# A hybrid diffusion trunk on one core: last states of a two-way scan left out, and row sums and spread scales by split products

## The chip, the core and the metric

The kernel runs on one core of a Trainium2 chip. The engines are named as the profile names them: PE (TensorE, matrix products), PEld (its weight loads), DVE (VectorE), ACT (ScalarE), POOL (GpSimd) and SP (SyncE, whose queue issues most DMAs). Each engine takes its own instructions in a fixed order, and semaphores make them wait for one another. The metric is the device time of one execution in microseconds (us).

## The reference, cut to what matters

One layer: an HGRN2 mixer (a gated linear recurrence, run forward and backward over the tokens), then a gated ConvFFN, each behind an RMS norm with shift, scale and gate from a conditioning vector. D = 1024, 2048 latent tokens and 256 context tokens, 8 heads of 128, everything float32. The scan, cut to its core:

```python
def hgrn2_chunk_scan(q, k, v, logf, s0):
    # S_t = diag(f_t) S_{t-1} + k_t v_t^T, o_t = S_t^T q_t, in chunks
    ...
    kv = einsum('bhnjk,bhnjv->bhnkv', k * exp(b_last - b), v)
    def step(s, inp):
        dcy, u = inp
        return dcy[..., None] * s + u, s
    s_final, s_start = lax.scan(step, s0, (decay, kv))
    o_inter = einsum('bhnik,bhnkv->bhniv', q * exp(b), s_start)
...
for d in range(2):
    oc_d, s_ctx = hgrn2_chunk_scan(<context, flipped if d>, s0)
    ol_d, _     = hgrn2_chunk_scan(<latents, flipped if d>, s_ctx)
...
sh1, sc1, g1, sh2, sc2, g2 = split(silu(c) @ w_ada + b_ada, 6)
```

A context scan gives its final state to the latent scan of the same direction. The final state of a latent scan (`_`) is read by nothing.

## The kernel before

**Products.** A float32 product of full precision is one PE instruction that the trace shows as two records. The large products are split instead: an operand `x` becomes `h` (an ACT copy rounded to float32r, line L89) and `l = x - h` (DVE, L90), and `x·y` is taken as three fast products `hh`, `hl`, `lh` (`mm3`, L520 to L522). Weights come from HBM into a float32 tile `raw` and are split from there.

**The scan** (`mixer_scan`, about the first 1285 us). Tokens are cut into tiles of 128 (two of context, -2 and -1, and 16 of latents, 0 to 15) and these into six units of three tiles, in two groups: {-2,-1,0}, {1,2,3}, {4,5,6} and {7,8,9}, {10,11,12}, {13,14,15}. The loops run over group, then head, then the three units. For a head, `load_head` brings five weight blocks of 128x1024 (types 1 and 2, the gates of the two directions, into `wh`/`wl`; types 0, 3, 4 into `vh`/`vl`). `unit` emits two gate products (24 matmuls of 384 columns each), q and three value products, and the elementwise scans on DVE. It returns `part_a` and `part_b` for its three tiles s, which are emitted inside the next unit: `part_a` transposes the keys of both directions (`tr`, copied to `kt`) and makes the scores (`sc`), `part_b` makes `kv`, the outputs `o`, and steps the forward state `Sf`; the backward increment `st[:, 2]`, the outputs and the queries go to `stash[t]` in DRAM. Later (`mixer_out`, `heads(t)` for t from 14 down to 0) the backward state `Sb` walks over the stash.

**What else runs in the scan.** `ada_rest` is a generator that makes four rows of the modulation: `acc` sums eight loads `raw` of 128x1024 on DVE, two full-precision products with a column of ones add up the partitions (L782, shape 1x512), ACT copies them to `row` (L783) and a DMA stores it to `m_row` (L784). From head 1 on each unit takes one step of it; a row takes 8 steps, so the products stand behind unit (head 3, 1) and unit (head 6, 0) of each group. `Hidden` prepares the normed tokens of a unit: `total` (`zs`), `root`, `spread0` (a diagonal matrix `dg` of scales) and `spread` (one full-precision product of 384 columns with ones, `zr`, L206).

**The two raw buffers.** The tiles `raw` of the weights and of `ada_rest`, and `row`, share one tag with two buffers in the pool `rawp`: a load may be issued when the tile before the last in that tag has been read for the last time. `wh`/`wl` hold one head: the next head's weights are split into them after the gate products of the head's third unit. A scheduler decides the order of instructions on each engine; SP's queue holds the loads and the stash writes in one order.

Of the kernel before, what the change touches and what calls it, by code (L numbers as in the profile page):

```python
# [10 lines left out]
F32R = mybir.dt.float32r  # L11
# [3 lines left out]
OP = mybir.AluOpType  # L15
# [42 lines left out]
def body(ctx, tc, a, out):  # L58
# [80 lines left out]
    wp = pool_(c1, "wp", 2)  # L139
    hq = pool_(c1, "hq")  # L140
    fix = pool_(c1, "fix")


    PLACE = {("h", 0): 0, ("l", 0): 1, ("h", 1): 2, ("l", 1): 3, ("l", 2): 4, ("h", 2): 5}
# [14 lines left out]
    class Hidden:  # L159
# [40 lines left out]
        def spread0(self):  # L200
            self.dg = self.xp.tile([128, NSC, 128], F32, name="dg", tag="dg")
            diag(self.dg, self.rs)

        def spread(self):
            z = self.ps.tile([128, 1, UN], F32, name="zr", tag="tr")
            pe.matmul(z[:, 0], ones, self.dg.rearrange("p s n -> p (s n)"), start=True, stop=True)  # L206
            self.z = z

        def scaled(self, g):
# [241 lines left out]
    def mixer_scan():  # L451
# [24 lines left out]
        def by_two(m):  # L476

            return m.rearrange("p (a c) b -> p c a b", c=2)

        mx, my, mw = mask("mx"), mask("my"), mask("mw")  # L480
        in_block(mx, 32)
        pool.tensor_copy(mw, mx)
# [41 lines left out]
        def unit(h, w, u, tiles, todo, begun=None, pace=6):  # L524
# [170 lines left out]

            kvb, kts, ats = [], {}, {}

            def part_a(s):
                g4 = slice(4 * s, 4 * s + 4)
                tr = ps.tile([128, 2, 128], F32, name="tr", tag="tr")  # L700
                for d in range(2):
                    pe.transpose(tr[:, d], kd[:, d, g4], ident)
                kt = gp.tile([128, 2, 128], F32, name="kt", tag="kt", bufs=3)
                act.activation(kt, tr, AF.Copy)
                kts[s] = kt
                if s < s0:
                    return

                sc = ps.tile([128, 3, 128], F32, name="sc", tag="sc", bufs=2)
                zig = [[64, 2], [(NS + 1) * 32, 2], [1, 32]]  # L710
                pe.matmul(sc[:, 0], kx[:, g4], walk(qp[:, 0, 4 * s], *zig), start=True, stop=True)
                for d in (1, 0):
                    qx = walk(qp[:, d, 4 * s + 1 - d], [(2 - d) * NS * 32, 2], [64, 2], [1, 32])
                    pe.matmul(sc[:, 2 - d], ke[:, d, g4], qx, start=True, stop=True)
                at = gp.tile([128, 128], F32, name="at", tag="at", bufs=2)
                af, ab = ABs[count["A"] % 2]
                count["A"] += 1
                act.activation(af[64:128, 0:64], sc[64:128, 1, 64:128], AF.Copy)
                act.activation(af[0:64, 64:128], sc[0:64, 2, 64:128], AF.Copy)
                dve.copy_predicated(ab, mxu, sc[:, 0])  # L720
                dve.copy_predicated(by_two(af.rearrange("p (a b) -> p a b", b=32)), myu,
                                    sc[:, 1:3, 0:64].rearrange("p c (a b) -> p c a b", b=32))
                dve.tensor_tensor(at, af, ab, OP.add)
                ats[s] = at

            def part_b(s):
                g4 = slice(4 * s, 4 * s + 4)
                kt = kts[s]
                kv = ps.tile([128, 2, 128], F32, name="kv", tag="kv")
                for d in range(2):  # L730
                    pe.matmul(kv[:, d], kt[:, d], v[:, s], start=True, stop=True)
                if s < s0:
                    kb = gp.tile([128, 3, 128], F32, name="kb", tag="st", bufs=4)
                    act.activation(kb[:, 0], kv[:, 1], AF.Copy)
                    kvb.append(kb[:, 0])
                    if s == 0:
                        dve.tensor_copy(Sf[:, h], kv[:, 0])
                    else:
                        dve.scalar_tensor_tensor(Sf[:, h], Sf[:, h], sd[:, 0, s:s + 1], kv[:, 0],
                                                 OP.mult, OP.add)  # L740
                        dve.scalar_tensor_tensor(Sb[:, h], kvb[1], sd[:, 1, 0:1], kvb[0],
                                                 OP.mult, OP.add)
                    return
                st = sts[s]
                o = ps.tile([128, 128], F32, name="o", tag="o")
                pe.matmul(o, qi[:, 0, g4], Sf[:, h], start=True, stop=False)
                pe.matmul(o, ats[s], v[:, s], start=False, stop=True)
                act.activation(st[:, 0], o, AF.Copy)
                act.activation(st[:, 2], kv[:, 1], AF.Copy)
                dve.scalar_tensor_tensor(Sf[:, h], Sf[:, h], sd[:, 0, s:s + 1], kv[:, 0],  # L750
                                         OP.mult, OP.add)
                t = tiles[s]
                if is_late(h, t):
                    pool.tensor_copy(st[:, 3], qi[:, 1, g4].rearrange("p g t -> p (g t)"))
                    return
                last = h == NH - 1 and t > NT - 4
                q_ = act if last else sp
                q_.dma_start(stash[t][:, 1, h], st[:, 0:2])
                q_.dma_start(stash[t][:, 0, h, 0], st[:, 2])
# [5 lines left out]
        def ada_rest():  # L765

            for i in range(4):
                acc = xp.tile([128, D], F32, name="acc", tag="acc")
                c = i * D
                for k in range(KT):  # L770
                    raw = rawp.tile([128, D], F32, name="raw", tag="raw")
                    sp.dma_start(raw, a["w_ada"][k * 128:(k + 1) * 128, c:c + D])
                    if k == 0:
                        dve.tensor_scalar(acc, raw, sil[:, k:k + 1], None, OP.mult)
                    else:
                        dve.scalar_tensor_tensor(acc, raw, sil[:, k:k + 1], acc, OP.mult, OP.add)
                    if k < KT - 1:
                        yield
                row = rawp.tile([1, D], F32, name="row", tag="raw")
                for n in range(2):  # L780
                    z = ps.tile([1, 512], F32, name="z", tag="pj", bufs=3)
                    pe.matmul(z, ones[:, 0:1], acc[:, n * 512:(n + 1) * 512], start=True, stop=True)  # L782
                    act.activation(row[:, n * 512:(n + 1) * 512], z, AF.Copy)  # L783
                sp.dma_start(m_rows[i], row)  # L784
                yield
# [67 lines left out]
        for g, units in enumerate(GROUPS):  # L853
            for h in range(NH):
# [4 lines left out]
                for u, tiles in enumerate(units):  # L859
# [3 lines left out]
                    if g == 1 and h == NH - 1 and u == 1:  # L863
                        more = last_tile()
                        todo += more[:3]
                    if h > 0 and steps < 16 * (g + 1):
                        next(rest, None)
                        steps += 1
                    if g == h == u == 0:
# [121 lines left out]
    def mixer_out(c3):  # L991
# [9 lines left out]
        def load_stash(i, t):  # L1001

            ko = wk2.tile([128, NH, 2, 128], F32, name=("kq", "og")[i], tag=("kq", "og")[i])
            for hs in ((slice(0, NH),) if t < NT - 3 else (slice(0, NH - 1), slice(NH - 1, NH))):
                sp.dma_start(ko[:, hs], stash[t][:, i, hs])
            return ko

        kqs, gts = {}, {}
# [1 line left out]
        def heads(t, between=()):  # L1010
# [15 lines left out]
            for hs, oi in zip(q4s, ois):  # L1026
# [2 lines left out]
                if between:  # L1029
                    between.pop(0)()  # L1030
                act.activation(oi, o, AF.Square)
            for h in range(NH):
                dve.scalar_tensor_tensor(Sb[:, h], Sb[:, h], decb[:, h, t:t + 1],
                                         kq[:, h, 0], OP.mult, OP.add)
            for hs, oi in zip(q4s, ois):
# [689 lines left out]
```

## Time and profile before

| | us |
|---|---|
| median of 3 runs | 2785.01 (2784.77 to 2789.52) |
| the profiled execution: its time | 2784.11 |
| its span, first to last instruction | 2782.4 |
| PE busy | 2756.6 (99%) |
| DVE busy | 2086.8 (75%) |
| ACT busy | 1155.7 (42%) |

The span is the time in which instructions ran; 1.7 us of the execution's time lie outside it. Busy time is the union of an engine's instructions; matmuls are pipelined, so that PE counts as busy as long as one is under way.

### The profile page before, as it was taken

Reading aid. Unit: us, or ns where it says so; the run is one execution under the profiler, and the core shown is the slowest. Engines: PE = TensorE matmul, PEld = TensorE weight load, DVE = VectorE, ACT = ScalarE, POOL = GpSimd, SP = SyncE. Lnnn points to the kernel's source line nnn. Section 1 sums busy time; section 2 is a strip of 40 time slices with the busy share of each in tenths; the row PEclk is TensorE's granted clock in tenths of the full one; section 3 lists DMA queues with packets and bytes.
Section 4 is the critical chain, followed back from the end, with each engine's and each line's share of the span. In section 5 each row is a group of like instructions: output and inputs, shape, how many; then the busy total and the mean of one; then the engine's idle time right before and its main releaser. Section 6 shows DMA issues by size and latency. Waiting matters only on the chain. (4 is left out here: it accounts for less than half of the span.)

```text
span 2782.4 us, 42929 instructions
## 1 busy us (share of the span) xinstructions
PE 2756.6 (99%) x15784; PEld 2477.7 (89%) x15784; DVE 2086.8 (75%) x3483; ACT 1155.7 (42%) x2424; POOL 598.5 (22%) x1012
## 2 busy tenths in 40 slices
PE   9999999999999999999999999999999999999999
PEld 8999999999999999998887888888888888887887
DVE  8766666577566665578997888887888887686887
ACT  6433333355333333333556444444444444333343
POOL 4111111111111111111111444433434431000001
PEclk9999999999999999999999999999999999999999
DMA  6322322212222322236788422326322224987653
GB/s 244 110 88 65 108 77 65 79 64 96 79 93 65 115 80 69 65 113 229 286 313 301 172 85 82 91 89 255 110 81 86 91 82 131 324 302 243 195 190 125
DMA packets 201755, 385.46 MB, mean 139 GB/s; under 512 B 26564, under 2 KB 118212, under 8 KB 196040
## 3 DMA queue, kind: packets, MB, share of 16 engines
q1 hardware_dynamic: 200968, 382.32, 40.8%
q8 instruction: 124, 2.03, 0.3%
q14 instruction: 87, 0.71, 0.1%
q10 hardware_dynamic: 576, 0.39, 0.0%
HBM read 280.65 MB, written 101.99 MB: 138 GB/s over the span
## 5 line engine op out<-in xcount | busy, mean ns | idle before, releaser
L520 PE MATMUL z<-vh,hh 128*128 128x256 f32 (+1 forms) x1024 | 300.5, 293 | 1.1 <-DVE q L593 1.1
L522 PE MATMUL z<-vh,hl 128*128 128x256 f32 (+1 forms) x1024 | 293.4, 287 | 0.0
L521 PE MATMUL z<-vl,hh 128*128 128x256 f32 (+1 forms) x1024 | 293.1, 286 | 0.0
L520 PE MATMUL z<-hh,wh 128*128 128x384 f32 x752 | 256.8, 342 | 0.0
L522 PE MATMUL z<-hh,wl 128*128 128x384 f32 x752 | 252.1, 335 | 0.0
L521 PE MATMUL z<-hl,wh 128*128 128x384 f32 x752 | 251.8, 335 | 0.0
L1554 PE MATMUL y<-wd,ml 128*128 128x512 f32 x600 | 233.8, 390 | 1.2 <-DVE ml L90 1.1
L1552 PE MATMUL y<-wd,mh 128*128 128x512 f32 x600 | 233.5, 389 | 0.0
L1553 PE MATMUL y<-wd,mh 128*128 128x512 f32 x600 | 233.5, 389 | 0.0
L637 POOL COPY TX<-S 128x3 f32<-128x3 f32 x48 | 32.1, 668 | 794.5 <-DVE S L601 794.5
L520 PEld LDWEIGHTS z<-vh,hh 128*128 128x128 f32 x1024 | 196.0, 191 | 1.8 <-DVE q L593 1.3
L521 PEld LDWEIGHTS z<-vl,hh 128*128 128x128 f32 x1024 | 196.1, 192 | 0.4
L522 PEld LDWEIGHTS z<-vh,hl 128*128 128x128 f32 x1024 | 195.7, 191 | 0.1
L90 DVE TENSOR_TENSOR w<-s,w 128x512 fp32r<-128x512 f32 x126 | 139.4, 1112 | 50.3 <-ACT w L89 50.2
L577 DVE TENSOR_TENSOR st<-z,st 128x128 f32<-128x128 f32 x127 | 36.7, 290 | 157.3 <-ACT st L576 157.3
L90 DVE TENSOR_TENSOR w<-raw,w 128x512 fp32r<-128x512 f32 x168 | 122.2, 730 | 39.6 <-ACT w L89 39.2
L572 ACT ACTIVATE v<-z 128x128 f32<-128x128 f32 x128 | 35.3, 276 | 278.6 <-PE z L522 278.5
L1300 DVE SCALAR_TENSOR_TENSOR r<-uv,conv,r 128x1023 f32<-128x1023 f32 (+1 forms) x88 | 148.3, 1704 | 0.4
L520 PEld LDWEIGHTS z<-hh,wh 128*128 128x128 f32 x752 | 141.6, 188 | 3.5 <-DVE st L577 2.6
L89 ACT ACTIVATE w<-raw 128x512 fp32r<-128x512 f32 x168 | 104.7, 628 | 94.0 <-PE zb L941 27.2
L521 PEld LDWEIGHTS z<-hl,wh 128*128 128x128 f32 x752 | 141.6, 188 | 0.0
L522 PEld LDWEIGHTS z<-hh,wl 128*128 128x128 f32 x752 | 141.2, 188 | 0.0
(371 smaller groups left out, 8006.0 us busy)
## 6 DMA issues: line engine op xcount, KB each, us to landing
raw<-in_w_up_dram SPq DMA_DIRECT2D x84, 512.0 KB, 3.7
raw<-in_w_in_dram SPq DMA_DIRECT2D x75, 512.0 KB, 3.7
lr<-m SPq DMA_DIRECT2D x49, 512.0 KB, 5.7
m<-r SPq DMA_DIRECT2D x66, 256.0 KB, 4.0
raw<-in_w_ada_dram SPq DMA_DIRECT2D x32, 512.0 KB, 4.8
stash<-st SPq DMA_DIRECT2D x125, 128.0 KB, 1.9
kq<-stash SPq DMA_DIRECT2D x13, 1024.0 KB, 7.9
og<-stash SPq DMA_DIRECT2D x13, 1024.0 KB, 7.0
```

Source lines behind the costliest of these rows:

```text
L89: act.activation(h, src, AF.Copy)
L90: dve.tensor_tensor(l, src, h.bitcast(F32), OP.subtract)
L520: pe.matmul(o, sh[:, k], mh[:, k], start=k == 0, stop=False)
L521: pe.matmul(o, sh[:, k], ml[:, k], start=False, stop=False)
L522: pe.matmul(o, sl[:, k], mh[:, k], start=False, stop=k == KT - 1)
L572: act.activation(v[:, s], z[:, 0:128], AF.Copy)
L577: dve.tensor_tensor(st[:, 1], z[:, 128:256], st[:, 1], OP.mult)
L637: pool.tensor_copy(TX[:, :, 1], tot[:, 0, :, 1])
L1300: dve.scalar_tensor_tensor(r, x, cw, r, OP.mult, OP.add)
L1552: pe.matmul(z, lh, rh, start=start, stop=False, skip_group_check=True)
L1553: pe.matmul(z, lh, rl, start=False, stop=False, skip_group_check=True)
L1554: pe.matmul(z, ll, rh, start=False, stop=stop, skip_group_check=True)
```

## The change

Three edits, all in or around the scan.

1. **End states.** `ways(s)` leaves direction 0 out at tile 15 and direction 1 at tile 0, in the transpose, the copy, `kv`, the state's step and the stash; `heads(0)` no longer steps `Sb`, and `load_stash` leaves out the part that is not written.
2. **Row sums.** `acc` is split into two float32r tiles `ap` in a step of its own (ACT, DVE); the next step takes four fast products with `ones_r`. A row now takes 9 steps, `steps < 18 * (g + 1)` instead of 16. The `ap` tiles are taken from the tag of `raw`.
3. **Spread.** Units 2 to 5 split `dg` into `dh`, `dl` and take two fast products instead of a full one.

```diff
+    ones_r = fix.tile([128, 128], F32R, name="ones_r")
...
             diag(self.dg, self.rs)
+            if self.unit > 1:
+                self.dgs = [self.xp.tile([128, NSC, 128], F32R, name=n, tag=n) for n in ("dh", "dl")]
+                split(*self.dgs, self.dg)
...
+            if self.unit > 1:
+                for i, d in enumerate(self.dgs):
+                    pe.matmul(z[:, 0], ones_r, d.rearrange("p s n -> p (s n)"),
+                              start=i == 0, stop=i == 1)
...
+        act.activation(ones_r, ones, AF.Copy)
...
+            def ways(s):
+
+                return range(tiles[s] == NT - 1, 1 if tiles[s] == 0 else 2)
+
...
-                for d in range(2):
+                for d in ways(s):
                     pe.transpose(tr[:, d], kd[:, d, g4], ident)
...
-                for d in range(2):
+                for d in ways(s):
                     pe.matmul(kv[:, d], kt[:, d], v[:, s], start=True, stop=True)
...
+                if t > 0:
+                    act.activation(st[:, 2], kv[:, 1], AF.Copy)
+                if t < NT - 1:
+                    dve.scalar_tensor_tensor(Sf[:, h], Sf[:, h], sd[:, 0, s:s + 1], kv[:, 0],
+                                             OP.mult, OP.add)
...
+                parts_ = [rawp.tile([128, D], F32R, name="ap", tag="raw") for _ in range(2)]
+                split(*parts_, acc)
+                yield
                 row = rawp.tile([1, D], F32, name="row", tag="raw")
                 for n in range(2):
                     z = ps.tile([1, 512], F32, name="z", tag="pj", bufs=3)
-                    pe.matmul(z, ones[:, 0:1], acc[:, n * 512:(n + 1) * 512], start=True, stop=True)
+                    for j, p in enumerate(parts_):
+                        pe.matmul(z, ones_r[:, 0:1], p[:, n * 512:(n + 1) * 512],
+                                  start=j == 0, stop=j == 1)
...
-                    if h > 0 and steps < 16 * (g + 1):
+                    if h > 0 and steps < 18 * (g + 1):
...
-            for h in range(NH):
+            for h in range(NH if t else 0):
```

The order of instructions at one place, the change from head 3 to head 4 in the first group, on three engines. The line numbers of the changed kernel differ (L805 is its row sum, L531 to L533 its `mm3`); the brackets name whose progress a row waits for (DMAHW numbers are lanes of DMAs).

PE before, from the last value product of unit (head 3, 2) on: `z_3743` and `z_3785` are the two gate products of head 4, `tr`, `sc`, `kv` belong to `part_a` and `part_b` of unit (head 3, 2).

```order
L520 MATMUL z_3743<-hh0_340,wh_3717 128x384 [waits DVE_49]
L521 MATMUL z_3743<-hl0_345,wh_3717 128x384
L522 MATMUL z_3743<-hh0_340,wl_3718 128x384
...
L702 MATMUL tr_3770<-ident_98,kd_3604 128x128 x2
L711 MATMUL sc_3775<-qp_3588,kx_3610 128x128
L714 MATMUL sc_3775<-qp_3588,ke_3581 128x128 x2
L520 MATMUL z_3785<-hh0_340,wh_3719 128x384 [waits DVE_49]
...
L702 MATMUL tr_3812<-ident_98,kd_3604 128x128 [waits Activation_49]
...
L711 MATMUL sc_3817<-qp_3588,kx_3610 128x128
```

PE now: `z_3701` and `z_3705` are the row sum, `z_3736` and `z_3778` the gate products of head 4.

```order
L805 MATMUL z_3701<-ap_3409,ones_r_128 1x512 [waits DVE_49]
L805 MATMUL z_3701<-ap_3410,ones_r_128 1x512
L805 MATMUL z_3705<-ap_3409,ones_r_128 1x512 [waits DVE_49]
L805 MATMUL z_3705<-ap_3410,ones_r_128 1x512
L717 MATMUL tr_3763<-ident_98,kd_3591 128x128 x2
L727 MATMUL sc_3768<-qp_3575,kx_3597 128x128
...
L763 MATMUL o_3823<-v_3509,at_3772 128x128 [waits DVE_49]
...
L763 MATMUL o_3885<-v_3509,at_3814 128x128 [waits DVE_49]
L531 MATMUL z_3736<-hh0_341,wh_3710 128x384 [waits Activation_49]
L532 MATMUL z_3736<-hl0_346,wh_3710 128x384
L533 MATMUL z_3736<-hh0_341,wl_3711 128x384 [waits DVE_49]
...
L533 MATMUL z_3778<-hh0_341,wl_3713 128x384 [waits DVE_49]
```

The row sum has moved from the end of unit (head 3, 1) to the end of unit (head 3, 2). Of that unit's `part_a` and `part_b` most now stands ahead of head 4's gate products, and these wait for ACT (`wh`) and DVE (`wl`). It is so at four places: heads 4 and 7 in both groups.

SP's queue before, for the loads of head 4: `raw_3723`, `raw_3727`, `raw_3731`, `raw_3735`, `raw_3739` are its types 1, 2, 0, 3, 4.

```order
L772 DMA raw_3714<-in_w_ada_dram 128x1024 [waits DMAHW6_49]
L784 DMA m_row0_60<-row_3418 1x1024 [waits DMAHW7_49,Activation_49]
L247 DMA raw_3723<-in_w_in_dram 128x1024 [waits DMAHW6_49,DMAHW0_49,DVE_49]
L247 DMA raw_3727<-in_w_in_dram 128x1024 [waits DMAHW7_49,DMAHW1_49]
L247 DMA raw_3731<-in_w_in_dram 128x1024 [waits DMAHW2_49,DMAHW0_49,DVE_49]
...
L247 DMA raw_3735<-in_w_in_dram 128x1024 [waits DMAHW5_49,DMAHW1_49,DVE_49]
...
L247 DMA raw_3739<-in_w_in_dram 128x1024 [waits DMAHW5_49,DVE_49]
```

SP's queue now: the same five are `raw_3716`, `raw_3720`, `raw_3724`, `raw_3728`, `raw_3732`.

```order
L257 DMA raw_3716<-in_w_in_dram 128x1024 [waits DMAHW3_49,PE_49]
L808 DMA m_row0_60<-row_3700 1x1024 [waits DMAHW4_49,Activation_49]
...
L778 DMA stash5_69<-st_3668 128x128 [waits DMAHW7_49,Activation_49]
L257 DMA raw_3720<-in_w_in_dram 128x1024 [waits DMAHW4_49,DMAHW0_49]
L257 DMA raw_3724<-in_w_in_dram 128x1024 [waits DMAHW3_49,DMAHW1_49,DVE_49]
...
L257 DMA raw_3728<-in_w_in_dram 128x1024 [waits DMAHW0_49,DVE_49]
...
L257 DMA raw_3732<-in_w_in_dram 128x1024 [waits DMAHW5_49,DMAHW1_49,DVE_49]
```

The load of type 1 now waits for PE, that is for the row sum that reads the `ap` tiles; the load of type 2 stands behind the row's store and a stash write of `st_3668`; the others wait for DVE, that is for the weight splits before them.

ACT before, around the first weight split for head 4.

```order
L555 ACTIVATE F1_548<-z_3426 128x12x32 [waits PE_49]
L704 ACTIVATE kt_3456<-tr_3453 128x256 [waits PE_49]
L718 ACTIVATE AB00_549<-sc_3458 64x64 [waits PE_49]
L719 ACTIVATE AB00_549<-sc_3458 64x64
L89 ACTIVATE wh_3717<-raw_3723 128x1024 [waits DMAHW0_49]
L89 ACTIVATE wh_3719<-raw_3727 128x1024 [waits DMAHW1_49,PE_49]
L555 ACTIVATE F1_548<-z_3468 128x12x32 [waits PE_49]
L704 ACTIVATE kt_3498<-tr_3495 128x256 [waits PE_49]
L718 ACTIVATE AB10_551<-sc_3500 64x64 [waits PE_49]
L719 ACTIVATE AB10_551<-sc_3500 64x64
L749 ACTIVATE st_3342<-kv_3510 128x128 [waits PE_49]
L748 ACTIVATE st_3342<-o_3513 128x128 [waits PE_49]
```

ACT now.

```order
L720 ACTIVATE kt_3869<-tr_3866 128x256 [waits PE_49]
L89 ACTIVATE wh_3710<-raw_3716 128x1024 [waits DMAHW3_49]
L734 ACTIVATE AB10_553<-sc_3871 64x64 [waits DVE_49,PE_49,Activation_49]
L735 ACTIVATE AB10_553<-sc_3871 64x64 [waits Activation_49]
L767 ACTIVATE st_3668<-kv_3882 128x128 [waits PE_49]
L764 ACTIVATE st_3668<-o_3885 128x128 [waits PE_49]
L89 ACTIVATE wh_3712<-raw_3720 128x1024 [waits DMAHW0_49]
L566 ACTIVATE F0_549<-z_3736 128x12x32 [waits PE_49]
```

The split of type 1 (`wh_3710`) now stands ahead of the copy that fills `st_3668`.

## Rows read from the trace of the kernel before

**Rows 1.** The page: span, busy time by engine, the chain by engine.
```profile
span 2782.4 us, 42929 instructions
...
PE 2756.6 (99%) x15784; PEld 2477.7 (89%) x15784; DVE 2086.8 (75%) x3483; ACT 1155.7 (42%) x2424; POOL 598.5 (22%) x1012
...
PE 39%; DMA 4%; DVE 2%; issue 1%; SPq 0%; ACT 0%; DVEq 0%; POOLq 0%; ACTq 0%
```

**Rows 2.** Waits of PE, 100 to 1200 us: total, times, longest.
```profile
PE o L746 <- DVE Sf L750: 0.6, 1, 0.6
```

**Rows 3.** Timeline of PE at a row sum: start us, us, operation, count.
```profile
297.60 1.88 PE L782 MATMUL z<-acc,ones 128*1 128x512 f32 x4
299.41 0.44 PE L520 MATMUL z<-hh,wh 128*128 128x384 f32 x1
```

**Rows 4.** Timeline of PE at the spread of unit 5.
```profile
648.49 0.71 PE L731 MATMUL kv<-v,kt 128*128 128x128 f32 x4
649.04 0.81 PE L206 MATMUL zr<-dg,ones 128*128 128x384 f32 x2
```

**Rows 5.** Timeline of PE: a gate product, then part_a and part_b.
```profile
308.59 0.34 PE L522 MATMUL z<-hh,wl 128*128 128x384 f32 x1
308.76 0.38 PE L702 MATMUL tr<-ident,kd 128*128 128x128 f32 x2
308.98 0.39 PE L711 MATMUL sc<-qp,kx 128*128 128x128 f32 x2
...
309.65 0.61 PE L731 MATMUL kv<-v,kt 128*128 128x128 f32 x4
310.10 0.39 PE L746 MATMUL o<-Sf,qi 128*128 128x128 f32 x2
```

**Rows 6.** Timeline of PE, fp32r products of 512 columns.
```profile
1533.73 0.39 PE L940 MATMUL zd<-rT,w 128*128 128x512 f32 x1
1533.96 0.40 PE L941 MATMUL zd<-rT,w 128*128 128x512 f32 x1
```

**Rows 7.** Line L89, 100 to 1190 us: ns min/median/max; ACT's waits.
```profile
L89 ACT ACTIVATE wh<-raw x28: 1047/1057/1060, 157.8 to 1167.8; 128x1024 fp32r<-128x1024 f32 x28
...
  PE z L521: 77.7, 25
```

**Rows 8.** Line L90, the same stretch.
```profile
L90 DVE TENSOR_TENSOR wl<-raw,wh x28: 1199/1226/1226, 158.8 to 1168.9; 128x1024 fp32r<-128x1024 f32 x28
```

**Rows 9.** Line L247, 150 to 1190 us: its DMAs and their us to landing.
```profile
L247 SPq DMA_DIRECT2D raw<-in_w_in_dram x68: 328/333/1123, 160.1 to 1187.9; - x68
...
DMA to landing us min/median/max: 3.4/3.6/5.8
```

**Rows 10.** The page's DMA issues: count, KB each, median us to landing.
```profile
raw<-in_w_ada_dram SPq DMA_DIRECT2D x32, 512.0 KB, 4.8
```

**Rows 11.** Tile m_row: us from issue to landing, all its DMAs.
```profile
DMA to landing us min/median/max: 3.5/3.8/4.8
```

**Rows 12.** Timeline of SP's queue around the change to head 4.
```profile
300.98 8.41 SPq L247 DMA_DIRECT2D raw<-in_w_in_dram  x3
...
328.91 0.33 SPq L247 DMA_DIRECT2D raw<-in_w_in_dram  x1
```

**Rows 13.** Timeline of ACT, the first weight split for head 4.
```profile
305.13 1.05 ACT L89 ACTIVATE wh<-raw 128x1024 fp32r<-128x1024 f32 x1
```

**Rows 14.** Groups of ACT by form, 150 to 1190 us: busy us, mean ns.
```profile
L749 ACT ACTIVATE st<-kv 128x128 f32<-128x128 f32 x108 | 29.6, 274 | 4.2 <-PE kv L731 3.9
L718 ACT ACTIVATE AB<-sc 64x64 f32<-64x64 f32 x108 | 23.6, 218 | 11.5 <-PE sc L714 5.1
...
L783 ACT ACTIVATE row<-z 1x512 f32<-1x512 f32 x8 | 4.7, 587 | 3.2 <-PE z L782 3.2
```

**Rows 15.** Windows: us, busy and count by engine, granted clock, DMA share, GB/s.
```profile
1255.00:1280.00 25.00, 22.33 (x171) 21.14 (x170) 20.32 (x55) 9.97 (x31) 3.72 (x9) 1.00 0.39 131
```

**Rows 16.** Groups of PE: the first of the program.
```profile
L334 PE MATMUL z<-dgs,ones 128*128 128x512 f32 x8 | 6.2, 946 | 4.0 <-DVE dgs L242 4.0
```

More of the change, by code (lines that the diff above doesn't have):

```diff
@@ L202, in spread0 @@
             diag(self.dg, self.rs)
+            if self.unit > 1:
+                self.dgs = [self.xp.tile([128, NSC, 128], F32R, name=n, tag=n) for n in ("dh", "dl")]
+                split(*self.dgs, self.dg)
         def spread(self):
             z = self.ps.tile([128, 1, UN], F32, name="zr", tag="tr")
-            pe.matmul(z[:, 0], ones, self.dg.rearrange("p s n -> p (s n)"), start=True, stop=True)
+            if self.unit > 1:
+                for i, d in enumerate(self.dgs):
+                    pe.matmul(z[:, 0], ones_r, d.rearrange("p s n -> p (s n)"),
+                              start=i == 0, stop=i == 1)
+            else:
+                pe.matmul(z[:, 0], ones, self.dg.rearrange("p s n -> p (s n)"),
+                          start=True, stop=True)
             self.z = z
@@ L700, in part_a @@
                 tr = ps.tile([128, 2, 128], F32, name="tr", tag="tr")
-                for d in range(2):
+                for d in ways(s):
                     pe.transpose(tr[:, d], kd[:, d, g4], ident)
                 kt = gp.tile([128, 2, 128], F32, name="kt", tag="kt", bufs=3)
-                act.activation(kt, tr, AF.Copy)
+                ds = slice(ways(s).start, ways(s).stop)
+                act.activation(kt[:, ds], tr[:, ds], AF.Copy)
                 kts[s] = kt
@@ L748, in part_b @@
                 act.activation(st[:, 0], o, AF.Copy)
-                act.activation(st[:, 2], kv[:, 1], AF.Copy)
-                dve.scalar_tensor_tensor(Sf[:, h], Sf[:, h], sd[:, 0, s:s + 1], kv[:, 0],
-                                         OP.mult, OP.add)
                 t = tiles[s]
+                if t > 0:
[3 more added lines that the diff above has]
+                                             OP.mult, OP.add)
                 if is_late(h, t):
@@ L758, in part_b @@
                 q_.dma_start(stash[t][:, 1, h], st[:, 0:2])
-                q_.dma_start(stash[t][:, 0, h, 0], st[:, 2])
+                if t > 0:
+                    q_.dma_start(stash[t][:, 0, h, 0], st[:, 2])
                 sp.dma_start(stash[t][:, 0, h, 1], qi[:, 1, g4].rearrange("p g t -> p (g t)"))
@@ L1004, in load_stash @@
             for hs in ((slice(0, NH),) if t < NT - 3 else (slice(0, NH - 1), slice(NH - 1, NH))):
-                sp.dma_start(ko[:, hs], stash[t][:, i, hs])
+                r = 0 if t or i else 1
+                sp.dma_start(ko[:, hs, r:], stash[t][:, i, hs, r:])
             return ko
```

## The prediction

> **What bounds the kernel now.** I read the page first: PE is busy for 2756.6 of the span's 2782.4 us, and the chain that ended last goes mostly along PE [rows 1]. Then the waits of PE over 100 to 1200 us, the stretch in which nearly all of the change lies: the list is headed by one wait of 0.6 us [rows 2]. So in the scan PE never stands still for longer than that. Two things follow. Whatever PE no longer has to do shortens the execution by just that much; and whatever makes PE wait, where it did not wait before, lengthens it by just that much. The other engines have room on the average, DVE at 75% and ACT at 42% [rows 1]. The profiled execution took 2784.11 us, 0.9 below the median of the runs shown, and all sums are made against it. 0.2% of it is 5.6 us: below 2779 I call it faster, above 2790 slower, and what lies between can hardly be told from no change.
>
> **What PE is relieved of.** *Row sums.* From the start of the two full products of one row to the next product PE takes 299.41 - 297.60 = 1.81 us [rows 3]. In their place stand four fast products of 512 columns. This form, with one output partition, does not occur before; the nearest row is a fast product of 512 columns with 128 output partitions, which starts 1533.96 - 1533.73 = 0.23 us before its successor [rows 6]. Four take 0.92, and four rows save 4 x (1.81 - 0.92) = 3.6 us. The bound on the other side is that a fast product of this form is no cheaper than a full one, 0.9: then the four rows cost 7 us more. I take the first, since the columns streamed are the same. *Spread.* The `kv` products ahead of it end at 648.49 + 0.71 = 649.20 and the product `zr` at 649.04 + 0.81 = 649.85, so it takes 0.65 [rows 4]. Two fast products of 384 columns take 2 x 0.17 (308.59 to 308.76) [rows 5], together 0.35. Four units (2 to 5) save 1.2. *End states.* A transpose takes (308.98 - 308.76) / 2 = 0.11 and a `kv` product (310.10 - 309.65) / 2 = 0.225 [rows 5]. For 8 heads and two directions, 16 of each go: 16 x 0.335 = 5.4. **Together 10.1 us less.**
>
> What the edits add elsewhere lies beside PE's work: four splits of 1024 columns (1.06 on ACT [rows 7], 1.23 on DVE [rows 8]), four of 384, one copy for `ones_r`, against 8 state copies, 8 steps of `Sf`, 8 of `Sb` and 8 stash writes fewer. I cost them at nothing. Their cover is PE's unbroken work; were it gone, the eight splits would be worth at most some 4 x 2.3 + 4 x 1.1, about 13 us.
>
> **What the row's ninth step moves.** The `ap` pair fills both buffers of `raw` from unit (head 3, 1) until the row sum at the end of unit (head 3, 2) has read it. The order of SP shows the consequence: head 4's load of type 1 now waits for PE. Before, this load was issued at 300.98 [rows 12], its split ran on ACT at 305.13 [rows 13], and such splits waited only for PE (25 of 28 [rows 7]): the weights lay ready. Now their whole way begins at the row sum. This happens four times, at heads 4 and 7 of both groups. I count one switch from the start of the row sum, with 0.05 to 0.1 for a hand-over between engines (my allowance).
>
> - Row sum 0 to 0.9, its tail and the hand-over: type 1 is issued at 1.2. A load takes 3.4 / 3.6 / 5.8 us, shortest, median, longest [rows 9]. It lands at 4.8, `wh` is ready at 5.9 [rows 7], `wl` at 7.15 [rows 8].
> - Meanwhile PE has what the order puts between: 6 transposes, and 17 of `sc`, `kv` and `o`, which I take at `kv`'s 0.225: 0.66 + 3.8 = 4.5 us, to 5.4. It waits 0.55 for `wh`, does two gate products (0.35), and waits another 0.9 for `wl`. **Idle 1.5** (1.6 in the second group, whose filling is 0.1 shorter). The first gate product, 24 matmuls of 0.175, ends at 11.05.
> - The load of type 2 stands in SP's queue behind the row's store and a stash write of `st_3668`, which ACT fills only after `wh` of type 1: two `AB` copies of 0.22 and one of 0.27 [rows 14] bring it to 6.9. The row's own copies (0.59 each [rows 14]) are done by 2.2, earlier than that, and the store (3.5 to 4.8 [rows 11]) blocks nothing behind it. Type 2 is issued at 7.2, lands at 10.8, is split at 11.9 and 13.1; **idle 1.1** in two pieces, and the second gate product ends at 17.0.
> - Type 0 gets the first buffer when `wl` of type 1 is done, is issued at 7.6 beside type 2, and lands at about 13.0 (5.4: above the 4.8 of a load among others [rows 10], within the longest). `vh` 14.1, `vl` 15.3. Type 3 gets the other buffer at 13.1: landed at 17.0, split by 18.1 and 19.3. Type 4 has to wait for `vl` of type 0: issued at 15.6, with 4.8 landed at 20.4, `vh` 21.5, `vl` 22.7. Before, this last one was issued at 328.91, 28 us after the first [rows 12]; now it is on the path.
> - In the first group PE goes from the gate products to a value product of 384 columns that needs type 4: **idle 21.6 - 17.0 = 4.6**, and the vt products of the context's values that follow its first matmul cover `vl`. In the second group the q product, which needs type 0 alone, comes first (24 x 0.175 = 4.2, to 21.2); what is left is 0.35 for `vh` and, as nothing lies between the value product's first two matmuls, about 1.0 for `vl`, **1.35**.
>
> A switch costs 1.5 + 1.1 + 4.6 = 7.2 us in the first group and 1.6 + 1.1 + 1.35 = 4.05 in the second; two of each are 22.5. **2784.1 - 10.1 + 22.5 = 2796.5.** From below: with all loads at 3.4 a switch costs 5.2 and 2.6, in all 15.6, and the time is 2789.6. From above: with 5.8 for the three loads that follow one another on the chain, each switch gets some 4 to 5 us more, and it is about 2815.
>
> **A rule on the clock.** Around waits that add up to 2.7 us in 25, PE's granted clock stayed at 1.00 [rows 15], which is 2.4 GHz. Only the program's first products look slower: 8 records in 6.2 us after an idle time of 4.0 [rows 16], 0.78 each, against 4 in 1.88, 0.47 each, of the same size inside the scan [rows 3]. The 4.6 us in which PE would do nothing at a switch of the first group is longer than any wait inside the scan before, and as long as that idle start. If the clock fell to its lower level, the 24 matmuls behind the wait would take twice 0.175, 4.2 more per switch: 2805 if it happens in the first group alone, 2813 at all four. The Trainium skill speaks for this: its page "TensorE: Matmul & The Clock Gate", section "HAM oscillation — how this bites in real kernels", tells of kernels whose array goes back to half rate in each wait for a transfer. By that rule the time is the higher one; no row of this scan shows such a wait yet.
>
> **The rivals.** *All waits are hidden* (faster). The time is 2774.0 if the weights come before PE needs them. For it speak 4.5 us of filling and the room on ACT and DVE; against it, that shortest load, split and hand-overs come to 1.2 + 3.4 + 1.06 + 1.23 = 6.9 us against 0.9 + 4.5 + 0.35 = 5.75 of PE's work, so 1.1 is lost even then. A gain over 0.2% needs less than 5.4 us lost, 1.35 per switch. Chance 0.06. *Only the first wait remains* (the same): later loads come sooner, since PE's delay gives them time, and 4 x 1.5 leave 2780; or more of the type 4 wait is hidden than I count. Against it stands the single chain of two buffers, type 0 to type 4. Chance 0.12. *The clock falls*, 2805 to 2813: 0.12. *My forecast*, 2796 with 2790 to 2804 of its own: 0.70. Within 0.2% are 0.12 and a sliver of the forecast's lower end; slower is 0.82. The range reaches from 2786, in the second rival's upper part, to 2811, which takes in most of the clock's case and the longer loads.
>
> **What would show it.** In the trace after: `tr` and `kv` with 272 and 544 records in place of 288 and 576, four records of fast products per row at 0.23 spacing, two for each `zr`, and PE's busy time lower by 10 us. PE's waits should list, where one of 0.6 was, L531 on ACT's `wh` and L533 on DVE's `wl` four times each for either gate, and L531 on `vh` twice at 4 to 5 us; SP should show loads that wait for PE. The granted clock should stay at 1.00 there. I am wrong if the type 4 weights land before the second gate product ends, if PE finds other work in those waits, or if the gaps are there and the second group makes them good later, which a PE without idle time cannot.

## The result and the profile after

The median is 2807.25 us (2804.79 to 2811.84, 5 runs) against 2785.76 of the kernel before beside it: 21.5 us slower, ratio 1.0078, interval 1.0067 to 1.0088. The profiled execution took 2804.79 us, 20.7 more than that of before.

The page of the changed kernel, where before stood [rows 1]:

```profile
span 2801.8 us, 42759 instructions
...
PE 2755.8 (98%) x15736; PEld 2476.0 (88%) x15736; DVE 2093.0 (75%) x3475; ACT 1158.8 (41%) x2426; POOL 601.4 (21%) x1012
```

The span has grown by 19.4 us and PE's busy time has fallen by 0.8. So PE stands still for 20.2 us more than it did. That its busy time fell by 0.8 and not by the 10.1 that it was to be spared says that a part of the work that is left took longer. The waits of PE, 100 to 1200 us (in total, times, longest), where one of 0.6 headed the list [rows 2]:

```profile
PE z L531 <- ACT vh L89: 6.9, 2, 3.6
PE z L531 <- ACT wh L89: 2.6, 3, 1.3
PE z L533 <- DVE wl L90: 2.5, 6, 0.7
PE zs L193 <- DVE sq L183: 1.4, 1, 1.4
```

There they are, the weights that come late: `vh` twice for over 3 us, `wh` and `wl`. The fourth switch lies beyond 1200; up to 1300 `wl` comes to 3.4 in 8 times, `wh` to 3.1 in 4, and the second wait for `vl` (L532) is 0.9 long. SP's queue at the change to head 4 (start us, us, operation, count), which answers to [rows 12]:

```profile
324.63 0.33 SPq L257 DMA_DIRECT2D raw<-in_w_in_dram  x1
325.49 0.28 SPq L808 DMA_DIRECT2D m_row<-row  x1
...
330.53 0.85 SPq L257 DMA_DIRECT2D raw<-in_w_in_dram  x2
...
336.93 0.33 SPq L257 DMA_DIRECT2D raw<-in_w_in_dram  x1
...
339.30 0.33 SPq L257 DMA_DIRECT2D raw<-in_w_in_dram  x1
```

The load of type 1 is issued at 324.63 in place of 300.98, those of types 2 and 0 at 330.53, type 3 at 336.93 and type 4 at 339.30, and the row's store lies between. PE at the row sum, which answers to [rows 3], and where it comes back from its wait for `vh`:

```profile
322.67 0.28 PE L533 MATMUL z<-vh,hl 128*128 128x256 f32 x1
322.79 0.28 PE L531 MATMUL z<-vh,hh 128*128 128x256 f32 x1
...
323.50 1.09 PE L805 MATMUL z<-ap,ones_r 128*1 128x512 f32 x4
324.43 0.38 PE L717 MATMUL tr<-ident,kd 128*128 128x128 f32 x2
```

```profile
344.64 0.69 PE L531 MATMUL z<-vh,hh 128*128 128x384 f32 x1 [3.58 <-ACT vh L89]
...
346.19 0.41 PE L533 MATMUL z<-hh,vl 128*128 128x256 f32 x1
346.40 0.41 PE L531 MATMUL z<-hh,vh 128*128 128x256 f32 x1
...
348.67 0.33 PE L531 MATMUL z<-vh,hh 128*128 128x384 f32 x1
348.85 0.33 PE L532 MATMUL z<-vl,hh 128*128 128x384 f32 x1
```

Four records of the row sum take 324.43 - 323.50 = 0.93 us (predicted 0.92). Ahead of 344.64 PE has done nothing for 3.58 us, and then its products of 256 columns stand 0.21 apart, where the same shape stood 0.12 apart before the switch (322.67 to 322.79). By 348.67 the spacing of the products of 384 columns is 0.17 to 0.18 again. The windows (us, busy and count by engine, granted clock, DMA share, GB/s) say why:

```profile
340.00:342.50 2.50, 1.06 (x7) 0.74 (x5) 1.93 (x5) 1.44 (x2) 0.71 (x2) 1.00 0.70 208
342.50:345.00 2.50, 0.36 (x1) 0.36 (x2) 2.27 (x4) 1.06 (x1) 0.52 (x3) 0.82 0.42 115
345.00:347.50 2.50, 2.50 (x12) 2.50 (x12) 2.07 (x5) 0.31 (x1) 2.44 (x8) 0.50 0.51 174
347.50:350.00 2.50, 2.50 (x16) 2.50 (x15) 1.56 (x4) 0.00 (x0) 0.73 (x1) 1.00 0.55 164
```

The granted clock, 1.00 until 342.50, is 0.50 from 345.00 to 347.50, the lower of its two levels (1.2 GHz), and 1.00 again after that. It fell shortly before the wait's end (1.00 in 343.50 to 344.00, 0.59 in 344.00 to 344.50), and the first dozen products behind the wait ran at half rate. At the switch to head 7 of the first group the same is seen behind a wait of 3.36, with 0.50 from 570 to 572.5; at the second group's switches, where no wait is longer than 0.9, the clock stays up. The rule of the Trainium skill that the prediction cites (page "TensorE: Matmul & The Clock Gate", section "HAM oscillation — how this bites in real kernels"), that the array goes back to half rate in a wait for a transfer, is borne out by these two waits of 3.58 and 3.36.

Where the time went can be read from the large split products (L531 to L533, before L520 to L522), of which both kernels have the same 6480 in the scan: how much later each starts than the one of the same number in the trace of before. The first starts 0.67 later. Two such pairs stand around the switch to head 4, one of the last value products ahead of it and the first gate product of the next unit, each time before and now:

```profile
323.15 0.28 PE L520 MATMUL z<-vh,hh 128*128 128x256 f32 x1
347.14 0.42 PE L520 MATMUL z<-hh,wh 128*128 128x384 f32 x1
```

```profile
320.63 0.28 PE L531 MATMUL z<-vh,hh 128*128 128x256 f32 x1
354.11 0.42 PE L531 MATMUL z<-hh,wh 128*128 128x384 f32 x1
```

The lag goes from -2.52 to 6.97. Over the other three switches it goes from 3.80 to 14.00, from 10.26 to 14.47 and from 11.91 to 16.46; between them it shrinks by about 0.36 with each head, the end states, and by 2 where before had its row sum. With the row sum (0.93) that now stands in each taken off, and the end state (0.34) that falls into the two switches of the second group added back, the switches cost 8.56, 9.27, 3.62 and 3.96, together 25.4. The scan ends 16.7 late, the span 19.4, the execution 20.7.

### The profile page after: what moved, and what is told of

The parts are those of the page before. It is cut to its first block, busy times and chain, and to the rows that moved or that the text cites. A ratio compares the mean times of both kernels' runs of the same rounds, so it can differ in the third digit from the quotient of the medians.

```text
span 2801.8 us, 42759 instructions
## 1 busy us (share of the span) xinstructions
PE 2755.8 (98%) x15736; PEld 2476.0 (88%) x15736; DVE 2093.0 (75%) x3475; ACT 1158.8 (41%) x2426; POOL 601.4 (21%) x1012
## 5 line engine op out<-in xcount | busy, mean ns | idle before, releaser
L531 PE MATMUL z<-vh,hh 128*128 128x256 f32 (+1 forms) x1024 | 299.7, 293 | 8.0 <-ACT vh L89 6.9
L532 PE MATMUL z<-vl,hh 128*128 128x256 f32 (+1 forms) x1024 | 293.7, 287 | 1.2 <-DVE vl L90 1.2
L533 PE MATMUL z<-vh,hl 128*128 128x256 f32 (+1 forms) x1024 | 293.2, 286 | 0.0
L531 PE MATMUL z<-hh,wh 128*128 128x384 f32 x752 | 256.6, 341 | 3.3 <-ACT wh L89 3.1
L533 PE MATMUL z<-hh,wl 128*128 128x384 f32 x752 | 252.8, 336 | 3.4 <-DVE wl L90 3.4
L532 PE MATMUL z<-hl,wh 128*128 128x384 f32 x752 | 251.7, 335 | 0.0
L531 PEld LDWEIGHTS z<-vh,hh 128*128 128x128 f32 x1024 | 196.1, 192 | 8.9 <-ACT vh L89 7.6
L532 PEld LDWEIGHTS z<-vl,hh 128*128 128x128 f32 x1024 | 196.2, 192 | 1.7 <-DVE vl L90 1.7
L533 PEld LDWEIGHTS z<-vh,hl 128*128 128x128 f32 x1024 | 196.0, 191 | 0.0
L90 DVE TENSOR_TENSOR w<-s,w 128x512 fp32r<-128x512 f32 x126 | 141.1, 1125 | 47.3 <-ACT w L89 47.3
L90 DVE TENSOR_TENSOR w<-raw,w 128x512 fp32r<-128x512 f32 x168 | 124.8, 745 | 38.0 <-ACT w L89 37.6
L533 PEld LDWEIGHTS z<-hh,wl 128*128 128x128 f32 x752 | 141.1, 188 | 5.4 <-DVE wl L90 5.4
L531 PEld LDWEIGHTS z<-hh,wh 128*128 128x128 f32 x752 | 141.5, 188 | 4.8 <-ACT wh L89 4.7
L89 ACT ACTIVATE w<-raw 128x512 fp32r<-128x512 f32 x168 | 104.7, 629 | 92.6 <-PE zb L965 27.2
L532 PEld LDWEIGHTS z<-hl,wh 128*128 128x128 f32 x752 | 141.5, 188 | 0.0
```

Of the source, the lines that this page charges most:

```text
L89: act.activation(h, src, AF.Copy)
L90: dve.tensor_tensor(l, src, h.bitcast(F32), OP.subtract)
L531: pe.matmul(o, sh[:, k], mh[:, k], start=k == 0, stop=False)
L532: pe.matmul(o, sh[:, k], ml[:, k], start=False, stop=False)
L533: pe.matmul(o, sl[:, k], mh[:, k], start=False, stop=k == KT - 1)
```

## The experiments

Each was timed in five rounds beside the kernel before, whose medians there were 2785.0 to 2786.2.

**1. The row's tiles in buffers of their own.**

```diff
-                parts_ = [rawp.tile([128, D], F32R, name="ap", tag="raw") for _ in range(2)]
+                ap = xp.tile([128, 2, D], F32R, name="ap", tag="xT")
+                parts_ = [ap[:, j] for j in range(2)]
...
-                row = rawp.tile([1, D], F32, name="row", tag="raw")
+                row = gp.tile([1, D], F32, name="row", tag="row", bufs=1)
```

> All three edits, but the ap pair and the row tile lie outside the tag of raw, so that a row sum holds no buffer of the weight loads. If the buffers cause the loss, the 10.1 us of PE work come through: 2785.8 - 10.1 = about 2776, ratio 0.9964, no waits for wh, wl or vh at heads 4 and 7, clock 1.00. Rival one, the ninth step itself (a row sum that stands at a head's end) costs, wherever its tiles lie: 2800 or more. Rival two, the edits save PE nothing: 2785.

Measured: 2783.56, ratio 0.9992 (0.9983 to 1.0000). PE's waits, 100 to 1200 us, are headed by these two:

```profile
PE zs L193 <- DVE sq L183: 2.2, 2, 1.9
PE qz L598 <- ACT kt L720: 1.8, 2, 1.5
```

No wait for `wh`, `wl` or `vh` at those switches is left, though the row sum stands at the head's end as in the changed kernel. The loss of 21.5 us needs the buffers. But of the 10.1 only some 2.6 are gained. PE ends the scan 3.2 early; one place that lost is seen on ACT (start us, us, instruction, and the idle time before it with what ended it):

```profile
267.06 1.06 ACT L89 ACTIVATE ap<-acc 128x1024 fp32r<-128x1024 f32 x1 [1.30 <-DVE acc L795]
268.03 0.26 ACT L581 ACTIVATE qt<-z 128x128 f32<-128x128 f32 x1
...
268.50 0.39 ACT L720 ACTIVATE kt<-tr 128x256 f32<-128x256 f32 x1
```

The split of `ap` waits for the last `acc` on DVE, and the copies of `qt`, `kt` stand behind it in ACT's order: PE waits 1.5 us for them, to 268.9. This is a split that I had costed at nothing. Around the end of the scan the clock fell in the profiled execution (0.71 in 1255 to 1260, 0.74 in 1275 to 1280), which at 2788.31 is also the longest of this run's eleven.

**2 and 8. One holder alone.** Run 2 is run 1 with the row back in the tag of `raw`; run 8 is the changed kernel with the row in `gp` and the pair in `raw`.

> All three edits; only the ap pair lies outside the tag of raw, the row tile still takes one of its two buffers. If the pair alone causes the loss: 2776. If the row tile, at the head's end now, holds up the load of type 2 as well (its buffer is free only when the row's store has landed, 4.4 to 5.9 us after issue in the changed kernel): type 1 is split in time, the rest of the chain is late, and about half the loss is left, 2785 to 2797. Rival, the ninth step itself: about 2807.

> All three edits with the ninth step where the change put it; the row tile lies outside the tag of raw, the ap pair stays in it (the mirror of the run in which only the pair lay outside, 2805). If either holder alone is enough to start the chain of five loads at the row sum: 2800 to 2810. If the row's store, which lands 4.4 to 5.9 us after issue, was the real hold and the pair's release by PE is early enough: 2785 to 2795.

Measured: 2805.09, ratio 1.0072 (1.0060 to 1.0085), with the row as the only holder, and 2800.31, ratio 1.0057 (1.0044 to 1.0069), with the pair. Either is enough for over two thirds of the loss (18.9 and 15.3 of 21.5 us), so the two do not add up. With the row as the only holder the interval overlaps that of the whole change: what the pair adds to it can't be told. "About half" for run 2 was too little. SP's queue in run 8, from the row's store on:

```profile
325.19 0.29 SPq L808 DMA_DIRECT2D m_row<-row  x1
325.92 0.36 SPq L257 DMA_DIRECT2D raw<-in_w_in_dram  x1
```

With the row elsewhere the load of type 2 leaves 0.7 us behind the store, at 325.92, and ahead of the stash writes, in place of 330.53; PE's wait for `wh` at this switch is gone, that for `vh` is still 3.07. So in the changed kernel it is the row's buffer, freed when its store has landed, that holds type 2 back.

**3. The ninth step alone, in the kernel before.**

```diff
+                yield
                 row = rawp.tile([1, D], F32, name="row", tag="raw")
...
-                    if h > 0 and steps < 16 * (g + 1):
+                    if h > 0 and steps < 18 * (g + 1):
```

> The kernel before with one thing added: a row takes nine steps, so that its two full products stand behind the third unit of heads 3 and 6. No ap pair, no split, no other edit. If only the pair costs: 2785.8, ratio 1.000. If the row tile in the tag of raw costs by itself: PE waits for type 2 and type 4 at four head switches and the time is 2792 to 2805.

Measured: 2806.61, ratio 1.0076 (1.0063 to 1.0089): slower by as much as the whole change, with no split, no pair and two full products for a row. It spares PE nothing, though: over the scan its lag grows by 21.4, while the four switches of the changed kernel cost 25.4 and its edits give 9.3 of that back. Its waits of PE, 100 to 1200 us, its SP queue at the same switch, and ACT there:

```profile
PE z L520 <- ACT vh L89: 6.3, 2, 3.2
PE z L520 <- ACT wh L89: 3.8, 3, 2.3
```

```profile
319.61 0.45 SPq L247 DMA_DIRECT2D raw<-in_w_in_dram  x1
326.07 0.29 SPq L785 DMA_DIRECT2D m_row<-row  x1
...
329.66 1.67 SPq L247 DMA_DIRECT2D raw<-in_w_in_dram  x2
...
339.48 0.33 SPq L247 DMA_DIRECT2D raw<-in_w_in_dram  x1
```

```profile
325.46 0.59 ACT L784 ACTIVATE row<-z 1x512 f32<-1x512 f32 x1 [0.27 <-PE z L783]
...
328.01 1.05 ACT L89 ACTIVATE wh<-raw 128x1024 fp32r<-128x1024 f32 x1
```

The load of type 1 goes out at 319.61, 4 us ahead of the row sum, since its buffer is free; but ACT takes its split only at 328.01, behind the row's copies and the work of `part_a`. Type 2 needs the buffer of `row` and leaves at 329.66, behind the row's store of 326.07. From there on the chain of loads through two buffers is that of the changed kernel: type 4 at 339.48, there 339.30.

**5 and 6. The row sum where it stood before.** Run 5 is the changed kernel with a row's nine steps begun one unit earlier; run 6 splits and multiplies in one step, so that a row takes eight.

```diff
-                    if h > 0 and steps < 18 * (g + 1):
+                    if (h > 0 or u == 2) and steps < 18 * (g + 1):
```

```diff
                 split(*parts_, acc)
-                yield
...
-                    if h > 0 and steps < 18 * (g + 1):
+                    if h > 0 and steps < 16 * (g + 1):
```

> The changed kernel, edit for edit, with the nine steps of a row begun one unit earlier (at the third unit of head 0 of each group), so that the row sums stand behind the second unit of heads 3 and 6, where they stood before; the ap pair and the row still take the two buffers of raw. If the moment of the row sum is what costs, the five loads of heads 4 and 7 have a whole unit again (some 25 us): no waits for wh, wl, vh, and 2776 to 2783, ratio 0.996 to 0.999. Rival, the pair in the tag of raw costs wherever the row sum stands: 2795 or more.

> The changed kernel with the split and the four fast products in one step, so that a row takes eight steps as before and its row sum stands behind the second unit of heads 3 and 6. The pair is held only from the split to the products, but PE comes to the products about 2.4 us (ACT 1.06, DVE 1.23) after the last load is added up. If the scheduler puts work between: 2776 to 2783. Rival, PE waits for the split at each of four rows: some 4 x 2 us more, 2784 to 2790.

Measured: 2782.87, ratio 0.9992 (0.9983 to 1.0000), and 2780.44, ratio 0.9981 (0.9972 to 0.9990). In both the pair and the row lie in the tag of `raw`. PE's waits in run 5, 100 to 1200 us, are headed by these two:

```profile
PE kv L747 <- DVE Sf L755: 0.9, 1, 0.9
PE zs L193 <- DVE sq L183: 0.7, 1, 0.7
```

So a tile in the tag of `raw` makes PE wait for no weights as long as a whole unit lies between the row sum and the head's end. Run 6 is the first that beats the kernel before by more than its interval. In both the scan ends 7.3 us early.

**4. Work in the waits.**

```diff
+            if s0 and h in (4, 7):
+                z = ps.tile([128, UN], F32, name="z", tag="pj", bufs=3)
+                for k in range(20):
+                    pe.matmul(z, feat[1][1][:, k % KT], vh[:, k % KT], start=k == 0, stop=k == 19)
             v = gp.tile([128, NSC, 128], F32, name="v", tag="v", bufs=2)
```

> The changed kernel, with 20 products of 384 columns (20 x 0.175 = 3.5 us) whose result nothing reads added between the gate products and the value products of heads 4 and 7 in the first group, where PE stood idle for 3.6 and 3.4 us and the granted clock then fell to 0.50. If the clock's fall is a part of the price, the clock stays at 1.00 there and the time falls by about 3 us, to 2804, with 7 us more of PE work. If the fall costs nothing: 2807. If the added work isn't hidden by the wait: 2811 or more.

Measured: 2805.64, ratio 1.0075 (1.0061 to 1.0088); beside the changed kernel's 1.0067 to 1.0088 that is no difference that can be told. The windows of the same place:

```profile
340.00:345.00 5.00, 5.00 (x32) 5.00 (x30) 3.60 (x6) 2.50 (x3) 0.65 (x2) 1.00 0.50 158
345.00:350.00 5.00, 4.50 (x27) 4.30 (x27) 3.38 (x7) 0.31 (x1) 3.24 (x10) 1.00 0.56 175
```

With PE at work there the clock stays at 1.00. 7 us of added products cost no time, which shows that the wait was idle through and through. Whether the clock's fall costs 3 us more the times can't tell, but the trace can. From the first product behind the wait to the next unit's first gate product PE takes 8.86 us (344.52 to 353.38) in place of 9.47 (344.64 to 354.11), and at head 7 10.15 in place of 10.96. So the two falls cost 0.6 and 0.8 us, 1.4 together and not 3: with the clock up PE meets a wait for `vl`, of 0.50 and 0.54, that it didn't have before.

```profile
345.70 0.44 PE L532 MATMUL z<-vl,hh 128*128 128x384 f32 x1 [0.50 <-DVE vl L90]
```

**7. Edits 1 and 3 alone**, without the split row sum and its step.

> Edits 1 and 3 alone: end states left out and spread by two fast products; row sums, their eight steps and buffers as before. By the terms of the sum PE has 5.4 + 1.2 = 6.6 us less to do: 2785.8 - 6.6 = 2779.2, ratio 0.9976. Rival, the copies and splits that come with them cost PE waits at the changes of units, and little or nothing is left: 2783 to 2787.

Measured: 2784.64, ratio 0.9996 (0.9987 to 1.0005). The end of the scan gained 5.6 against its first unit (that one 1.3 later than before, the last 4.3 earlier), close to the sum; then it was given back: at the last tile of `mixer_out` (near 1485) PE waited 3.1 us for `gl`, 0.6 before, and the clock was low behind it.

**9, 10 and 12. What gives the gain back at the last tile.** Run 9 is run 6 with the eight steps of `Sb` in `heads(0)` put back on other data; run 10 is the kernel before without these steps; run 12 is run 9 with the part of the stash at tile 0 that edit 1 left out written (with other data) and loaded again.

```diff
-            for h in range(NH if t else 0):
+            for h in range(NH):
                 dve.scalar_tensor_tensor(Sb[:, h], Sb[:, h], decb[:, h, t:t + 1],
-                                         kq[:, h, 0], OP.mult, OP.add)
+                                         kq[:, h, 0 if t else 1], OP.mult, OP.add)
```

```diff
-                r = 0 if t or i else 1
-                sp.dma_start(ko[:, hs, r:], stash[t][:, i, hs, r:])
+                sp.dma_start(ko[:, hs], stash[t][:, i, hs])
```

> The run in which split and products stand in one step (2780.4), with the eight steps of Sb in heads(0) put back on DVE; they run on other data (the queries) and nothing reads what they leave. If the order that DVE's instructions took when these eight left (two weight splits of 0.69 between the og steps and gl, PE's wait for gl 1.9 to 3.4 us in place of 0.6, and the clock low behind it) is what gave the gain back: gl is waited for less than 1 us, the clock stays high there, and 2776 to 2778.5. Rival, the eight steps are in nobody's way and leaving them out costs nothing: 2780.4 again.

> The kernel before with one thing left out: the eight steps of Sb in heads(0), on DVE, whose result nothing reads. Eight instructions fewer and none added. If the order is what costs: slower, 2786 to 2790, with a wait for gl of 1.4 to 3.4 us at the last tile of mixer_out. Rival, it costs nothing: 2785.0, with the wait at 0.6 as before.

> The run with split and products in one step and the steps of heads(0) kept (2780.55), with one more thing as before: the part of the stash that edit 1 left out at tile 0 is written again (with other data, eight writes of 64 KB) and loaded again, so that the load kq of tile 0 is one of 1024 KB and SP's queue near the end of mixer_out stands in the order of before (og of tile 1 behind two stores, not right behind kq). If the place of these loads is what makes PE wait 2.8 us for gl at the last tile and drops the clock behind it: a wait under 1 us, the clock high at 1480, 2776 to 2778.5. Rival, the wait comes from the 8 us that the scan is shorter by, with the order of the loads no part of it: 2780.5 again.

Measured: 2780.55, ratio 0.9984 (0.9975 to 0.9993); 2784.96, 0.9997 (0.9988 to 1.0006); 2781.15, 0.9983 (0.9974 to 0.9992). The order of DVE's steps is not what costs: runs 9 and 10 stand where they stood without that edit. The waits of PE and the windows near the last tile, first of run 9, then of run 12:

```profile
PE y L1090 <- DVE gl L90: 2.8, 1, 2.8
```

```profile
1480.00:1485.00 5.00, 2.44 (x6) 1.97 (x7) 4.91 (x13) 4.09 (x10) 0.00 (x0) 0.79 0.71 273
1485.00:1490.00 5.00, 5.00 (x24) 4.09 (x23) 2.61 (x5) 1.59 (x5) 0.56 (x1) 0.87 0.63 186
```

```profile
PE y L1088 <- DVE gl L90: 0.6, 1, 0.6
```

```profile
1480.00:1485.00 5.00, 4.42 (x20) 3.44 (x19) 3.07 (x6) 3.92 (x10) 0.00 (x0) 1.00 0.74 300
1485.00:1490.00 5.00, 5.00 (x28) 4.19 (x27) 3.92 (x8) 2.73 (x6) 0.56 (x1) 1.00 0.46 100
```

In the trace of run 12 the wait is back at 0.6, the clock stays up, and the profiled execution took 2777.75, 6.4 less than that of before. Yet the median isn't lower than run 9's. The 11 timed executions of run 12 lie between 2776.7 and 2785.7, so something else that one profile doesn't show makes many of them longer. My theory on the loads explains the trace and not the median. One candidate, tested by no run, is a fall of the clock that comes in some executions and not in others: the profile of run 12 shows none around the scan's end and the last tile, that of run 6 shows 0.67 in 1270 to 1275 and 0.66 in 1485 to 1490.

**11. Run 9 without the spread edit.**

> The run with split and products in one step and the steps in heads(0) kept, without edit 3: the spread stays one full product. If the two fast products save the 1.2 us of my sum: 1.2 slower than with them. Rival, the copy and the subtraction that stand ahead of the product give it back (PE waited 0.3 to 0.4 for dh): the same or faster, by under 1 us.

Measured: 2782.80, ratio 0.9990 (0.9981 to 0.9999), 2.2 us above run 9, with intervals that overlap. It leans to a gain from the two fast products. The traces say how much: between 541 and 712 us of before's time, around the change of groups, where three of the four spreads lie, PE of run 9 gains 1.0 on before and that of run 11 loses 0.2. That is 1.2 where three spreads were to save 0.9; it is one trace each.

## Why the prediction was right, and where it was not

- **That PE bounds the scan**, so that each wait at a switch is paid in full: it held. What ran late there was never made good.
- **The work spared.** Row sums came out as worked out (0.93 for four, 0.92 predicted), end states too (0.36 per head and direction, 0.335 predicted), and the two fast products of a spread (0.35, 599.57 to 599.92 in the changed kernel, 0.35 predicted). The switches cost 25.4 and the lag grows by 16.0 over the scan, so that 9.3 of the 10.1 came through in the changed kernel. In runs 6 and 12 PE had gained 9.7 and 9.0, counted from its first large product, by the last unit's gate products; at the end of the scan 8.3 were left of either, since PE waits 2.4 and 1.8 for `q` in the last unit (1.05 before). In runs 5 and 9 it is 7.9, with waits of 1.9 for `Sf` (near 74) and 1.5 for `kt` (near 269) that before doesn't have. So the term is right but for 1 to 2 us of waits for ACT and DVE, which I had costed at nothing.
- **The cause of the waits** is the step that failed in part. I put the late loads down to the `ap` pair, which fills both buffers, and the wait of type 2 to a stash write ahead of it in SP's queue; the row's store, I wrote, blocks nothing behind it. In the changed kernel type 1 does wait for the pair (324.63, right behind the row sum). But run 3 has no pair and loses as much, run 2 has the row alone and loses nearly as much, and run 8 shows that type 2 waits for the row's buffer. What is needed is a row sum at the end of a head with any of its tiles, the row alone too, in the tag of the weight loads. Run 1 takes the tiles out and run 5 the moment, and both are rid of it.
- **The price of a switch**, 7.2, 7.2, 4.05 and 4.05 in the prediction, was 8.6, 9.3, 3.6 and 4.0: 25.4 against 22.5. That the sum is near is in good part luck, since its errors cancel. The waits that I counted add up to 14.8 only: the first wait of each switch was 0.65 to 0.8 (predicted 1.5), the second 0.8 to 1.5 (1.1), the third 3.6 and 3.4 (4.6) in the first group and 0.3 and 0.9 (1.35) in the second. The other 10.6 stand nowhere in my sum. Some 3 of it is the clock, by the spacing of the products at the two switches (by run 4, 1.4 that the clock alone costs; in the rest PE would have waited for `vl`). What is left is gaps that I had not thought of: `part_a` and `part_b` of a unit now follow each other with no gate products between, so that `o` waits for `at` (summed from start to start, the `o` products with `at` take 1.0 and 0.9 us more over the third and the fourth switch), and a gate product behind a wait is followed after 0.28 in place of 0.17 (330.75 to 331.03).
- **The clock rival** came true, at just the two switches that it named and at a lower price: some 3 us and not 8.4, since a dozen of the 24 products behind each wait ran at half rate. A chance of 0.12 was too low for waits that I had myself put at 4.6 us. The median lies in that rival's 2805 to 2813, above my likeliest case's own 2790 to 2804, but the clock alone doesn't carry it there. The profiled execution lies 8.3 above the 2796.5 of the sum: 2.9 by the switches with the clock in them, some 0.8 by work that was not spared, and 4.7 that lie outside the scan.
- **What I costed at nothing.** Of these 4.7, 0.7 lie at the start, 2.7 behind the scan (PE's waits there add up to 8.4 in place of 6.0), 1.3 outside the span. At the start it is the copy for `ones_r`, which ACT now takes first. ACT before, then now:

```profile
0.80 1.28 ACT L272 ACT_TABLE_LOAD   x1 [0.80 <-PEq L1716]
2.72 0.22 ACT L272 ACTIVATE sil<-vec 128x16 f32<-128x16 f32 x1 [0.64 <-DMA vec<-in_vecs_dram]
```

```profile
2.10 0.31 ACT L490 ACTIVATE ones_r<-ones 128x128 fp32r<-128x128 f32 x1
2.42 1.28 ACT L282 ACT_TABLE_LOAD   x1
3.72 0.21 ACT L282 ACTIVATE sil<-vec 128x16 f32<-128x16 f32 x1
```

A second table load of 1.28 us stands between the copy and `sil`, and PE's first product starts at 4.99 in place of 4.00; it is 4.99 or 5.00 in every run with `ones_r` and 3.96 to 4.02 without. In runs 5, 6, 7, 9 and 11, too, between 1.9 and 3.4 us go in a wait for `gl` at the last tile; run 12 points to the smaller load of tile 0, which stands elsewhere in SP's order, without showing it in the median.
- **The signs.** `tr` and `kv` have the 272 and 544 records that I named, and PE waits for `wl` eight times as I named, but for `wh` four times and not eight. PE's busy time fell by 0.8 and not by 10, and the clock did not stay up.

A version that beats both kernels is run 6 (2780.44): all three edits, with the split and the products of a row in one step.

## What to carry to other kernels

A tile that shares a tag with streamed loads is a place in their queue: before a step is moved, ask for each of its tiles, the smallest too, which load comes next in that tag and how much time it has. Moving the step by one unit cost 25.4 us at the switches where all the edits spared PE 9.3, and moving it back was as good as more memory. And a wait of some microseconds on the bounding engine should be priced with the slower clock behind it, less what that engine would have waited for next in any case.

## What the runs showed of the hardware

- In waits of 3.4 and 3.6 us of the changed kernel PE's granted clock fell to 0.50, and the first products behind them ran at that; behind the other waits at its switches, up to 1.3, it stayed at 1.00. At the last tile the length of the wait doesn't tell: 2.8 us in run 9 went with a fall (0.79 and 0.87 in two windows of 5 us), 1.9 in run 6 too (0.66), and 2.8 in run 1 with none (1.00 from 1480 to 1495).
- A copy of 0.31 us on ACT ahead of `sil` went with a second table load of 1.28 us, and PE's first product came 1.0 later.
- Executions of one kernel spread more than I expected: 2776.0 to 2784.8 for run 6 and 2776.7 to 2785.7 for run 12, 11 each. An edit worth 2 us is seen in a trace and hardly in a median.
